# Two layers of a gated-recurrence and dilated-attention model: SwiGLU weights moved by 64 bytes in their tiles, one more pair of hidden columns computed by seven products

## The chip, the core and the metric

The kernel runs on one core of a Trainium2 chip. The metric is the device time of one launch in microseconds (us), lower is better. TensorE (PE) multiplies matrices and loads their stationary operand (PEld), VectorE (DVE) and ScalarE (ACT) do elementwise work, GpSimd (POOL) some additions and reductions, and SyncE (SP) issues most transfers from memory.

## The reference

512 tokens of width 1024 go through two layers in float32. Layer 0 mixes tokens by a gated recurrence (HGRN2), layer 1 by dilated attention; each is followed by a SwiGLU feed-forward part (FFN) with 2816 hidden columns.

```
cond = silu(c)
for layer in range(2):
    mod = cond @ ada_w[layer] + ada_b[layer]
    sh1, sc1, g1, sh2, sc2, g2 = split(mod, 6)
    u = rms_norm(h, norm_g[layer, 0]) * (1 + sc1) + sh1
    y = hgrn2_mixer(u, ...) if layer == 0 else dilated_attention_mixer(u, ...)
    h = h + (1 + g1) * rms_norm(y, norm_g[layer, 1])
    u = rms_norm(h, norm_g[layer, 2]) * (1 + sc2) + sh2
    gate, up = split(u @ ffn_w_in[layer], 2)          # 1024 -> 2 x 2816
    y = (silu(gate) * up) @ ffn_w_out[layer]          # 2816 -> 1024
    h = h + (1 + g2) * rms_norm(y, norm_g[layer, 3])
```

## The kernel before

Every float32 operand is split into two parts, hi (the value rounded by ScalarE's cast) and lo (the rest, by a VectorE subtraction). `three` (L401 to L404) replaces one product by three matmuls on the same PSUM bank: hi by hi, hi by lo, lo by hi. The first operand is the stationary one (the weights), the second the moving one (the tokens, `uh` and `ul`, tiles of 128 x 8 x 512).

**Weights.** A `Stream` loads the weights in the order in which they are needed, through SP's queue: 1 MB pieces [128, 2048] into two `raw` buffers. `process_to` casts each into a `hi` tile (L83, ACT) and subtracts into a `lo` tile (L84, DVE); there are three buffers of each. Between the weights the stream carries pieces of `ada_w` (the table that `cond` is multiplied with). Most of these are summed by VectorE (L241, L243), the total over the partitions by POOL's all-reduce (L245); `row_fin` (L290, L291) then needs two short rows, `ada_b` and `norm_g` (loads of L59). For layer 0's values 2 to 4 PE does it instead (L221), with a tile `tiled_cond` of copies of `cond` as its moving operand, which DVE fills at L1300. An equal tile, `cond_tiles`, exists earlier in the start stage, in a pool that has been closed by then.

**FFN.** The 2816 hidden columns are 22 blocks f of 128. `PLAIN = (4, 2)` says how many pairs of blocks each layer computes in the plain way: a pair is 4 products (gate and up, two blocks each) with 24 matmuls of 512 tokens, so 96 matmuls. Silu is L876, the product with up L877. The other blocks (f 8 to 21 in layer 0, f 4 to 21 in layer 1) go through `seven_products`: gate and up of one f are seen as a 2 x 2 block matrix and computed with seven block products (Strassen-like) instead of eight, each a `run` of 12 matmuls of 256 tokens, 84 matmuls for an f.

- Three of the runs use three quarters of the raw weights (tiles R: `spare` for even f, tiles of the stream's `hi` and `lo` rings for odd f), with the token parts B11, T4 and B21. R is cast by L746 on ACT, its lo part is L750 on DVE.
- Four use sums of the quarters (tiles Sm), with t2, T3, t1 and B22. The sums are made by L754 (POOL), L758 and L762 (DVE), cast by L770 (ACT, two halves) and subtracted by L774 (DVE, two halves).
- B11, B21 and B22 are slices of `uh`/`ul`; t1, T3, T4 and t2 are the token sums, in tiles `th`/`tl`, which `token_sums` makes once per layer (L711 to L718).
- L799, L803, L809, L814 on DVE and L833, L843, L810 on ACT combine the seven results.

One f is 4 transfers of 256 KB (L56, "quarters"). Those of the first f take the `raw` buffer that becomes free two pieces earlier.

**Order of the work.** Inside `tc.manual_schedule(engines=ORDERED)` PE, ACT, DVE and POOL run the instructions in the order of the code; `seven_products` is written so. Elsewhere a scheduler picks the order, so also for `token_sums`, for the plain pairs, for the casts of the stream's weights and for the FFN's second product.

**Places in SBUF.** As the program is laid out, the tiles `uh`, `ul`, `hi`, `lo` and `spare` begin 64 bytes past a multiple of 128 bytes in each partition, `th` and `tl` on a multiple of 128 bytes.

Of the kernel before, what the change touches and what calls it, by code (L numbers as in the profile page):

```python
# [15 lines left out]
P = 128  # L16
# [14 lines left out]
C3 = float(np.float32(TWO_PI - C1 - C2))  # L31
MAGIC = 12582912.0


# [116 lines left out]
def block_kernel(tc, x, c, positions, ada_w, ada_b, norm_g, hgrn_w_in, lower, hgrn_norm_g, hgrn_w_out,  # L151
# [6 lines left out]
    with ExitStack() as ctx:  # L158
# [49 lines left out]

        tiled_cond = []
        by_pe = lambda l, v: l == 0 and v in (2, 3, 4)  # L210

        def ada_groups(l, v, hf, kq):


            def run(raw):
                if kq == 0:
                    accs[l, v, hf] = bank("mm")
                ps, r = accs[l, v, hf], V4(raw)
                for k in range(4):
                    j = slice(32 * k, 32 * k + 32)  # L220
                    pe.matmul(ps[j], tiled_cond[0][:, kq * 4 + k], r[:, k], start=kq == 0, stop=kq == 1,  # L221
                              tile_position=(0, 32 * k))
# [118 lines left out]

        PLAIN = (4, 2)

# [362 lines left out]
        def token_sums(th, tl, room):  # L706

            q = lambda a, k: a[:, k // 2 * 4:k // 2 * 4 + 4, k % 2 * 256:k % 2 * 256 + 256].bitcast(F32)
            t = [room[:, 2 * k:2 * k + 2].rearrange("p a (b n) -> p (a b) n", b=2) for k in range(4)]
            for k in (0, 1, 3, 2):  # L710
                dve.tensor_add(t[k], q(uh, k), q(ul, k))  # L711
            dve.tensor_sub(t[0], t[0], t[1])
            dve.tensor_sub(t[1], t[3], t[1])
            dve.scalar_tensor_tensor(t[3], t[0], -1.0, t[3], op0=OP.mult, op1=OP.subtract)
            dve.scalar_tensor_tensor(t[2], t[3], -1.0, t[2], op0=OP.mult, op1=OP.subtract)
            for k in (3, 0, 2, 1):
                act.copy(th[:, k], t[k])
                dve.tensor_sub(tl[:, k], t[k], th[:, k].bitcast(F32))  # L718

        def seven_products(fs, mid, sgp, spare, th, tl):  # L720
# [5 lines left out]
            u_of = lambda r, c: [(uh[:, r * 4 + k, c * 256:c * 256 + 256], ul[:, r * 4 + k, c * 256:c * 256 + 256]) for k in range(4)]  # L726
            t_of = lambda i: [(th[:, i, k], tl[:, i, k]) for k in range(4)]
            B11, B21, B22 = u_of(0, 0), u_of(1, 0), u_of(1, 1)
# [14 lines left out]
            def r_hi(i):  # L743
                if i < len(fs):
                    raw[i] = st.quarters()
                    act.copy(places(i)[0][0][:, 0:1536], raw[i][:, 512:])  # L746

            def r_lo(i):
                hi, lo = places(i)[0]
                dve.tensor_sub(lo[:, 0:1536], raw[i][:, 512:], hi[:, 0:1536].bitcast(F32))  # L750

# [26 lines left out]

            def run(ps, w, k, us):
                for kt in range(4):  # L780
                    a = slice(k * 512 + kt * P, k * 512 + (kt + 1) * P)
                    three(ps, w[0][:, a], w[1][:, a], *us[kt], kt == 0, kt == 3)

            def runs(i):
# [8 lines left out]
                run(half(2, 1), Sm, 2, T3)  # L793
                run(half(2, 0), Sm, 1, t1)
                run(half(3, 0), Sm, 3, B22)

# [367 lines left out]
        with tc.manual_schedule(engines=ORDERED):  # L1164
# [6 lines left out]
            cT = fresh(sp, [P, 8], "cT", 1)  # L1171
            cond_tiles = sp.tile([P, KT, 32], F32, name="cond_tiles")
            busy(4)
# [124 lines left out]
        sc = cx.enter_context(tc.tile_pool(name="h_briefest", bufs=1))  # L1298
        tiled_cond.append(sc.tile([P, KT, 32], F32, name="tiled_cond"))
        dve.tensor_scalar(tiled_cond[0], cond.unsqueeze(2).broadcast_to((P, KT, 32)), 1.0 / 32, None, op0=OP.mult)  # L1300
        causal = sc.tile([P, P], F32, name="causal")
# [170 lines left out]

        cx.close()
        first = mixer_out(oT, otp, (8,), gates.pop((0, 2)), 0, "left", lambda: None)

# [260 lines left out]
```

## Time and profile before

| what | value |
|---|---|
| median of three runs | 1528.15 us (1527.87 to 1528.92) |
| profiled execution: its time | 1527.97 us |
| profiled execution: its span | 1526.3 us, so 1.67 us lie around it |
| granted TensorE clock | 0.998 |
| PE busy | 1507.9 us (99%) |
| DVE busy | 1010.5 us (66%) |
| ACT busy | 685.2 us (45%) |
| POOL busy | 233.3 us (15%) |
| matmuls | 8871 |

In a timeline row stand the start in us, the duration, the engine, the line, the operation, output <- inputs, how many, and in brackets the idle time before it with what ended it. Names are those of the program without buffer numbers. A matmul's duration covers its whole passage through the array; since they overlap, the pace is read from one start to the next. An SPq row of several issues shows the time from the first issue to the last.

### The profile page before, as it was taken

To read this page: it belongs to the slowest core of one execution; us is meant where nothing else is said; L and a number is where in the kernel's file an instruction comes from. 1 tells how busy PE (TensorE), PEld (TensorE's weight loads), DVE (VectorE), ACT (ScalarE), POOL (GpSimd) and SP (SyncE) were. 2 spreads that over 40 slices of the span, in tenths; PEclk is the share of its full clock that TensorE was granted. 3 is DMA by queue.
4 is the path that set the end of the run, shared out by engine and by line. 5 is a ranking of instruction groups with operands and counts; after the bars stand their busy time and mean duration, and the time that the engine had idled before them with its cause. 6 is when DMAs were issued, how large, how long until landed. Compare 5 with 4: busy or idle time off the path is not lost.

```text
span 1526.3 us, 22515 instructions
## 1 busy us (share of the span) xinstructions
PE 1507.9 (99%) x8871; PEld 1322.7 (87%) x8871; DVE 1010.5 (66%) x1737; ACT 685.2 (45%) x1091; POOL 233.3 (15%) x204
## 2 busy tenths in 40 slices
PE   8999999999999999999999999999999999999998
PEld 6777888898899988889888888988888999999886
DVE  4587866487688887462567686335656868888633
ACT  4433443362344533362456664245645534444231
POOL 1011210031122211140010111010002212221100
PEclk9999999999999999999999999999999999999999
DMA  9654443126433356414534433443202333334531
GB/s 307 184 160 135 156 138 111 56 84 207 125 109 106 108 198 221 151 55 139 165 99 133 130 111 111 138 111 84 83 30 82 106 89 110 104 107 151 186 117 55
DMA packets 203352, 192.77 MB, mean 126 GB/s; under 512 B 6584, under 2 KB 162416, under 8 KB 203248
## 3 DMA queue, kind: packets, MB, share of 16 engines
q1 hardware_dynamic: 201712, 190.87, 40.6%
q8 instruction: 69, 1.13, 0.3%
q0 software_dynamic: 1024, 0.13, 0.2%
q10 hardware_dynamic: 512, 0.35, 0.1%
q14 instruction: 35, 0.29, 0.1%
HBM read 189.17 MB, written 2.16 MB: 125 GB/s over the span
## 4 chain that ended last, share of the span: by engine, by line
PE 90%; DVE 3%; ACT 2%; issue 2%; DMA 1%; POOL 1%; DVEq 0%; POOLq 0%; ACTq 0%
PE ps_mm L402 20%; PE ps_mm L404 20%; PE ps_mm L403 20%; PE ps_b L402 3%; PE ps_b L404 3%; PE ps_b L403 3%; PE ps_a L404 3%; PE ps_a L403 3%; PE ps_a L402 3%; PE ps_mm L1140 1%; PE ps_a L1140 1%; PE ps_mm L221 1%; PE ps_a L1587 1%; PE ps_b L1140 1%; PE ps_a L1569 1%
## 5 line engine op out<-in xcount | busy, mean ns | idle before, releaser
L402 PE MATMUL ps_mm<-uh,hi 128*128 128x512 f32 (+1 forms) x816 | 309.8, 380 | 0.0
L404 PE MATMUL ps_mm<-uh,lo 128*128 128x512 f32 (+1 forms) x816 | 308.3, 378 | 0.0
L403 PE MATMUL ps_mm<-ul,hi 128*128 128x512 f32 (+1 forms) x816 | 307.4, 377 | 0.0
L84 DVE TENSOR_TENSOR lo<-raw,hi 128x2048 fp32r<-128x2048 f32 x78 | 186.0, 2384 | 168.0 <-ACT hi L83 167.8
L83 ACT CAST hi<-raw 128x2048 fp32r<-128x2048 f32 x78 | 148.8, 1908 | 172.0 <-DMA raw<-in_ffn_w_out_dram 53.4
L402 PEld LDWEIGHTS ps_mm<-uh,hi 128*128 128x128 f32 x816 | 153.8, 188 | 35.2 <-issue 8.4
L404 PEld LDWEIGHTS ps_mm<-uh,lo 128*128 128x128 f32 x816 | 153.8, 188 | 27.2
L403 PEld LDWEIGHTS ps_mm<-ul,hi 128*128 128x128 f32 x816 | 153.8, 189 | 26.2
L402 PE MATMUL ps_mm<-hi,oh 128*128 128x512 f32 x240 | 94.0, 392 | 0.0
L403 PE MATMUL ps_mm<-lo,oh 128*128 128x512 f32 x240 | 93.5, 390 | 0.0
L243 DVE SCALAR_TENSOR_TENSOR shared<-raw,cond,shared 128x512 f32<-128x512 f32 x98 | 73.4, 749 | 29.1 <-DMA raw<-in_ada_w_dram 27.4
L770 ACT CAST hiq<-raw 128x1024 fp32r<-128x1024 f32 x64 | 64.4, 1050 | 62.8 <-DVE raw L758 62.8
L245 POOL PARTITION_ALL_REDUCE shared<-shared x14 | 47.5, 3396 | 288.7 <-DVE shared L243 288.6
L404 PE MATMUL ps_mm<-hi,ul 128*128 128x512 f32 x192 | 76.0, 396 | 0.0
L403 PE MATMUL ps_mm<-lo,uh 128*128 128x512 f32 x192 | 75.9, 396 | 0.0
L774 DVE TENSOR_TENSOR loq<-raw,hiq 128x1024 fp32r<-128x1024 f32 x64 | 75.5, 1220 | 0.6 <-ACT hiq L770 0.6
L402 PE MATMUL ps_mm<-hi,uh 128*128 128x512 f32 x192 | 74.6, 396 | 0.0
L404 PE MATMUL ps_mm<-hi,ol 128*128 128x512 f32 x176 | 68.5, 389 | 0.0
L754 POOL TENSOR_TENSOR raw<-raw 128x512 f32<-128x512 f32 x32 | 52.5, 1642 | 99.4 <-DVE spare L750 42.4
L758 DVE TENSOR_TENSOR raw<-raw 128x1024 f32<-128x1024 f32 x32 | 39.2, 1226 | 36.7 <-POOL raw L754 36.5
L402 PE MATMUL ps_a<-hi,oh 128*128 128x512 f32 x152 | 59.7, 392 | 0.0
L403 PE MATMUL ps_a<-lo,oh 128*128 128x512 f32 x152 | 59.2, 390 | 0.0
(403 smaller groups left out, 3716.0 us busy)
## 6 DMA issues: line engine op xcount, KB each, us to landing
raw<-in_ada_w_dram SPq DMA_DIRECT2D x40, 1024.0 KB, 5.2
raw<-in_ffn_w_in_dram SPq DMA_DIRECT2D x128, 256.0 KB, 4.3
raw<-in_attn_w_in_dram SPq DMA_DIRECT2D x48, 512.0 KB, 4.9
raw<-in_ffn_w_out_dram SPq DMA_DIRECT2D x22, 1024.0 KB, 4.8
raw<-in_hgrn_w_in_dram SPq DMA_DIRECT2D x12, 1024.0 KB, 5.6
raw<-in_ffn_w_in_dram SPq DMA_DIRECT2D x12, 1024.0 KB, 5.1
raw<-in_attn_w_in_dram SPq DMA_DIRECT2D x12, 1024.0 KB, 5.2
first<-in_ada_w_dram SPq DMA_DIRECT2D x14, 512.0 KB, 7.6
```

Source lines behind the costliest of these rows:

```text
L83: self.nc.scalar.copy(hi, t)
L84: self.nc.vector.tensor_sub(lo, t, hi.bitcast(F32))
L243: dve.scalar_tensor_tensor(a, r[:, k], sc, a, op0=OP.mult, op1=OP.add)
L245: pool.partition_all_reduce(a, a, P, bass.bass_isa.ReduceOp.add)
L402: pe.matmul(ps, ah, bh, start=start, stop=False)
L403: pe.matmul(ps, ah, bl, start=False, stop=False)
L404: pe.matmul(ps, al, bh, start=False, stop=stop)
L754: pool.tensor_add(r[:, 2], r[:, 2], r[:, 0])
L758: dve.tensor_tensor(r[:, 0:2], r[:, 0:3:2], r[:, 1:2].broadcast_to((P, 2, 512)), op=OP.add)
L770: act.copy(hi, src)
L774: dve.tensor_sub(lo, src, hi.bitcast(F32))
L1140: pe.matmul(vbanks[hf, t], a, w, start=e == 0 and which == 0, stop=e == KT - 1 and which == 2)
```

## The change

1. The three raw quarters R begin R0 = 16 floats (64 bytes) later in their tiles (L746, L750, the three `run` calls), so on a multiple of 128 bytes. The token sums move from `th`/`tl` into `sums` (t1, T3, t2, on a multiple of 128 bytes) and `fourth` (T4, 64 bytes past one). `uh`, `ul` and Sm stay, 64 bytes past one. So in six of the seven runs of an f the stationary operand and the moving one now differ by 64 modulo 128, and only B22's are equal; before, they differed in four (T4, t2, T3, t1) and were equal in the three with `uh` (B11, B21, B22).
2. `PLAIN` becomes (3, 2): layer 0 has three plain pairs and 16 blocks by seven products (14 before).
3. `token_sums` stands inside `manual_schedule`, so the engines run it in the order of the code.
4. `tiled_cond` and its instruction go; `cond_tiles` lives on in a pool of its own until the first mixer is done, and L221 reads that.

```
+R0 = 16
+        tcx = ctx.enter_context(ExitStack())
+        cond_tiles = tcx.enter_context(tc.tile_pool(name="tiled", bufs=1, side="right")).tile([P, KT, 32], F32, name="cond_tiles")
...
-                    pe.matmul(ps[j], tiled_cond[0][:, kq * 4 + k], r[:, k], start=kq == 0, stop=kq == 1,
+                    pe.matmul(ps[j], cond_tiles[:, kq * 4 + k], r[:, k], start=kq == 0, stop=kq == 1,
...
-        PLAIN = (4, 2)
+        PLAIN = (3, 2)
...
-                act.copy(th[:, k], t[k])
-                dve.tensor_sub(tl[:, k], t[k], th[:, k].bitcast(F32))
+                act.copy(th[k], t[k])
+                dve.tensor_sub(tl[k], t[k], th[k].bitcast(F32))
...
-                    act.copy(places(i)[0][0][:, 0:1536], raw[i][:, 512:])
+                    act.copy(places(i)[0][0][:, R0:R0 + 1536], raw[i][:, 512:])
...
-                dve.tensor_sub(lo[:, 0:1536], raw[i][:, 512:], hi[:, 0:1536].bitcast(F32))
+                dve.tensor_sub(lo[:, R0:R0 + 1536], raw[i][:, 512:], hi[:, R0:R0 + 1536].bitcast(F32))
...
-            def run(ps, w, k, us):
+            def run(ps, w, o, us):
...
-                    a = slice(k * 512 + kt * P, k * 512 + (kt + 1) * P)
+                    a = slice(o + kt * P, o + (kt + 1) * P)
...
-                run(half(0, 0), R, 0, B11)
-                run(half(3, 1), R, 1, T4)
-                run(half(1, 0), R, 2, B21)
+                run(half(0, 0), R, R0, B11)
+                run(half(3, 1), R, R0 + 512, T4)
+                run(half(1, 0), R, R0 + 1024, B21)
                 run(half(1, 1), Sm, 0, t2)
...
-                    spare = [qp.tile([P, 3 * 512], F32R, name=f"spare{l}{k}") for k in range(2)]
-                    qp.tile([P, 112], F32, name=f"pad_q{l}")
-                    th = qp.tile([P, 4, 4, 256], F32R, name=f"th{l}")
-                    tl = qp.tile([P, 4, 4, 256], F32R, name=f"tl{l}")
+
+                    spare = [qp.tile([P, R0 + 1536 + n], F32R, name=f"spare{l}{n}") for n in (112, 96)]
+                    three_t = qp.tile([P, 2 * 3072 + 16], F32R, name=f"sums{l}")
+                    fourth_t = qp.tile([P, 2 * 1024], F32R, name=f"fourth{l}")
+                    K4 = lambda t: t.rearrange("p (k n) -> p k n", k=4)
+                    sums = [[K4(three_t[:, o + k:o + k + 1024]) for k in (0, 1024, 2048)] for o in (0, 3072)]
+                    for k in range(2):
+                        sums[k].insert(2, K4(fourth_t[:, k * 1024:(k + 1) * 1024]))
+                    th, tl = sums
...
-                            token_sums(th, tl, midt[:, NF - 8:])
+                            with tc.manual_schedule(engines=ORDERED):
+                                token_sums(th, tl, midt[:, NF - 8:])
...
-        tiled_cond.append(sc.tile([P, KT, 32], F32, name="tiled_cond"))
-        dve.tensor_scalar(tiled_cond[0], cond.unsqueeze(2).broadcast_to((P, KT, 32)), 1.0 / 32, None, op0=OP.mult)
```

Lines of the code after the change have numbers one to eight higher (L84 becomes L85, L746 L748, L774 L776, L877 L884).

On SP's queue, at the end of layer 0's plain pairs, the order before, from the last piece of `ada_w` for this stage:

```order
L65 DMA raw_3149<-in_ada_w_dram 128x4x512
L65 DMA raw_3210<-in_ffn_w_in_dram 128x8x256
L65 DMA raw_3217<-in_ffn_w_in_dram 128x8x256
L59 DMA raw_3223<-in_ada_b_dram 128x512
L59 DMA raw_3223<-in_norm_g_dram 128x512
L56 DMA raw_3280<-in_ffn_w_in_dram 128x4x128 x4
L56 DMA raw_3343<-in_ffn_w_in_dram 128x4x128 x4
```

And after:

```order
L66 DMA raw_3153<-in_ada_w_dram 128x4x512
L60 DMA raw_3214<-in_ada_b_dram 128x512
L60 DMA raw_3214<-in_norm_g_dram 128x512
L57 DMA raw_3222<-in_ffn_w_in_dram 128x4x128 x4
L57 DMA raw_3229<-in_ffn_w_in_dram 128x4x128 x4
```

The two 1 MB loads of the fourth pair are gone, and the quarters of the first f follow the rows at once; their `raw` buffer is the one of the `ada_w` piece in the first row.

On VectorE, around layer 0's token sums (L711 to L718, now L713 to L720), before:

```order
L713 TENSOR_TENSOR mid_3029<-mid_3029 128x1024
L243 SCALAR_TENSOR_TENSOR shared<-raw_2752,cond,shared 128x512
L718 TENSOR_TENSOR tl_3040<-mid_3029,th_3039 128x1024
L877 TENSOR_TENSOR mid_3029<-ps_mm_2757,sg_3044 128x512
L714 SCALAR_TENSOR_TENSOR mid_3029<-mid_3029 128x1024
L243 SCALAR_TENSOR_TENSOR shared<-raw_2752,cond,shared 128x512
L718 TENSOR_TENSOR tl_3040<-mid_3029,th_3039 128x1024
L84 TENSOR_TENSOR lo_3070<-raw_2922,hi_3069 128x2048
L715 SCALAR_TENSOR_TENSOR mid_3029<-mid_3029 128x1024
L718 TENSOR_TENSOR tl_3040<-mid_3029,th_3039 128x1024
L243 SCALAR_TENSOR_TENSOR shared<-raw_3067,cond,shared 128x512
L718 TENSOR_TENSOR tl_3040<-mid_3029,th_3039 128x1024
```

And after:

```order
L715 TENSOR_TENSOR mid_3031<-mid_3031 128x1024
L884 TENSOR_TENSOR mid_3031<-ps_mm_2759,sg_3045 128x512
L716 SCALAR_TENSOR_TENSOR mid_3031<-mid_3031 128x1024
L245 SCALAR_TENSOR_TENSOR shared<-raw_2754,cond,shared 128x512
L717 SCALAR_TENSOR_TENSOR mid_3031<-mid_3031 128x1024
L85 TENSOR_TENSOR lo_3074<-raw_2924,hi_3073 128x2048
L720 TENSOR_TENSOR sums_3040<-mid_3031,sums_3040 128x1024 x2
L720 TENSOR_TENSOR fourth_3041<-mid_3031,fourth_3041 128x1024
L720 TENSOR_TENSOR sums_3040<-mid_3031,sums_3040 128x1024
L245 SCALAR_TENSOR_TENSOR shared<-raw_3071,cond,shared 128x512 x2
```

The four subtractions that fill the sums' lo parts now stand together behind the weight's subtraction (L84, now L85), ahead of the next `ada_w` piece's sums; before they were spread.

On ScalarE, at the end of layer 0's seven products, before, from the cast of the last f's R to the first weight of the FFN's second product (L83):

```order
L746 CAST hiq_3472<-raw_4676 128x1536
L810 ACTIVATE shared<-shared 128x512
L833 COPY shared<-ps_mm_4791 128x256
L770 CAST hiq_3474<-raw_4676 128x1024 x2
L843 COPY shared<-ps_mm_4793 128x256
L83 CAST hi_5018<-raw_4786 128x2048
```

And after:

```order
L748 CAST hiq_3358<-raw_4782 128x1536
L812 ACTIVATE shared<-shared 128x512
L835 COPY shared<-ps_mm_4897 128x256
L84 CAST hi_5124<-raw_4892 128x2048
L772 CAST hiq_3360<-raw_4782 128x1024 x2
L845 COPY shared<-ps_mm_4899 128x256
```

The weight's cast now stands ahead of the two casts of the last f's Sm; on VectorE its subtraction (L84, now L85) in the same way stands ahead of the two L774 (now L776) of that f. The `hi` buffer that it writes is the one that held the Sm of the f before.

More of the change, by code (lines that the diff above doesn't have):

```diff
@@ L726, in seven_products @@
             u_of = lambda r, c: [(uh[:, r * 4 + k, c * 256:c * 256 + 256], ul[:, r * 4 + k, c * 256:c * 256 + 256]) for k in range(4)]
-            t_of = lambda i: [(th[:, i, k], tl[:, i, k]) for k in range(4)]
+            t_of = lambda i: [(th[i][:, k], tl[i][:, k]) for k in range(4)]
             B11, B21, B22 = u_of(0, 0), u_of(1, 0), u_of(1, 1)
@@ L788, in runs @@
                 half = lambda n, k: b[n][:, k * 256:k * 256 + 256]
[L789 to L791 removed]
+                run(half(0, 0), R, R0, B11)
+                run(half(3, 1), R, R0 + 512, T4)
+                run(half(1, 0), R, R0 + 1024, B21)
                 run(half(1, 1), Sm, 0, t2)
[L793 to L795 removed]
+                run(half(2, 1), Sm, 1024, T3)
+                run(half(2, 0), Sm, 512, t1)
+                run(half(3, 0), Sm, 1536, B22)
             def sums_1(i):
@@ L1171, in block_kernel @@
             cT = fresh(sp, [P, 8], "cT", 1)
-            cond_tiles = sp.tile([P, KT, 32], F32, name="cond_tiles")
             busy(4)
@@ L1473, in block_kernel @@
         cx.close()
+        tcx.close()
         first = mixer_out(oT, otp, (8,), gates.pop((0, 2)), 0, "left", lambda: None)
```

1 line of the change is left out of this document (removed).

## The prediction

> **What bounds the kernel now.** I read the page's busy times first, then TensorE's timeline, its idle gaps, and the other engines' timelines beside those places that the change touches.
>
> ```profile
> PE 1507.9 (99%) x8871; PEld 1322.7 (87%) x8871; DVE 1010.5 (66%) x1737; ACT 685.2 (45%) x1091; POOL 233.3 (15%) x204
> ```
>
> TensorE is busy for 99% of the span, so time comes or goes in three ways only: fewer or shorter matmul slots, a gap of TensorE closed, or a new gap. The unit for the first is the pace from start to start in layer 0's feed-forward part.
>
> ```profile
> 339.24 0.40 PE L402 MATMUL ps_mm<-uh,hi 128*128 128x512 f32 x1
> ...
> 404.55 0.28 PE L402 MATMUL ps_mm<-uh,spare 128*128 128x256 f32 x1
> ...
> 405.98 0.29 PE L402 MATMUL ps_mm<-th,spare 128*128 128x256 f32 x1
> ...
> 407.36 0.28 PE L402 MATMUL ps_mm<-uh,spare 128*128 128x256 f32 x1
> ...
> 408.78 0.29 PE L402 MATMUL ps_mm<-th,hiq 128*128 128x256 f32 x1
> ...
> 412.88 0.28 PE L402 MATMUL ps_mm<-uh,hiq 128*128 128x256 f32 x1
> ...
> 424.06 0.28 PE L402 MATMUL ps_mm<-uh,spare 128*128 128x256 f32 x1
> ```
>
> From 339.24 to 404.55 stand three plain pairs, 3 x 96 matmuls of 512 tokens: 65.31 us, 21.77 a pair, 0.2268 a matmul, and half of it, 0.1134, is the pace that 256 tokens would have at the same rate. From 404.55 to 424.06 stand two blocks f by seven products: 19.51 us, 9.755 a block. Inside one, the runs of 12 matmuls are not alike: B11 with `uh` takes 1.43, T4 with `th` 1.38, B21 with `uh` 1.42, and the three runs t2, T3, t1 with `th` 4.10 together, 1.367 each. So `uh` costs 0.05 to 0.06 a run more than `th`, at the same shapes.
>
> **The change part by part**, against the profiled execution's 1527.97 us, which is 0.18 under the median of the runs (1528.15); I make no correction for that.
>
> *The 64 bytes.* Before, `uh` and the weights both begin 64 bytes past a multiple of 128, while `th` and the weights differ by 64. All slow runs are of the first kind and all fast ones of the second. After the change B11, T4, B21, t2, T3 and t1 are all of the second kind, B22 stays of the first. Six runs at 12 x 0.1134 = 1.361 and one at 1.43 make 9.60 for a block: 0.155 less, for the 32 blocks that the kernel has already 5.0 us less. The ends: 0, if it is `uh` itself that is slow and not its place against the weights; and what VectorE allows at the other end. VectorE's wait on TensorE in a block is the 0.20 us of L809 that is quoted with the end of the stage below, so its own round is 9.755 - 0.20 = 9.555, and 32 x 0.20 = 6.4 is the most that the pace can give. I take 5.0, since slow and fast rows part exactly along the placement. It is also close to VectorE's limit: 0.05 us of slack a block is left.
>
> The Trainium skill, "SBUF — State Buffer", section "SBUF: two separate sides", says of TensorE that it never waits on anyone for its ports, and the page's table of bandwidths gives the weight load a second, independent read port. By that, the place of the operands could not change the pace, and the sum would lack these 5.0 us. The rows above show a difference between equal shapes that the rule has no word for; that it comes from the placement no row shows, since `uh` is never seen at another place.
>
> *One more pair by seven products.* 21.77 go, 2 x 9.60 = 19.20 come: 2.57 less (2.26 less without the shift, 21.77 - 19.51).
>
> *The copies of the condition.*
>
> ```profile
> 74.79 0.39 PE L1140 MATMUL ps_b<-late,uh 128*128 128x512 f32 x1
> 76.51 1.06 PE L221 MATMUL ps_mm<-raw,tiled_cond 128*32 128x512 f32 x8 [1.33 <-DVE tiled_cond L1300]
> ```
> ```profile
> 75.83 0.39 DVE L1300 TENSOR_SCALAR tiled_cond<-cond 128x256 f32<-128x256 f32 x1
> ```
> ```profile
> 69.67 0.37 SPq L65 DMA_DIRECT2D raw<-in_ada_w_dram  x1
> ```
> ```profile
> raw<-in_ada_w_dram SPq DMA_DIRECT2D x40, 1024.0 KB, 5.2
> ```
>
> L221 waited 1.33 us for the tile that the change removes. What is late next is its own piece of `ada_w`: issued at 69.67, with 5.2 us to landing, there at 74.9, before TensorE ends the matmul of 74.79 at 75.2. So 1.3 less; the ends are 1.33 and 0.3, should that piece land 1 us late.
>
> *The start of layer 0's seven products.* Here the fourth pair was the cover.
>
> ```profile
> 368.56 0.38 SPq L65 DMA_DIRECT2D raw<-in_ada_w_dram  x1
> 369.88 7.46 SPq L65 DMA_DIRECT2D raw<-in_ffn_w_in_dram  x2
> ...
> 387.98 5.94 SPq L56 DMA_DIRECT2D raw<-in_ffn_w_in_dram  x8
> ```
> ```profile
> 393.44 1.48 ACT L746 CAST spare<-raw 128x1536 fp32r<-128x1536 f32 x1 [9.39 <-DMA raw<-in_ffn_w_in_dram]
> ```
> ```profile
> 373.84 3.11 DVE L243 SCALAR_TENSOR_TENSOR shared<-raw,cond,shared 128x512 f32<-128x512 f32 x4 [3.98 <-DMA raw<-in_ada_w_dram]
> ...
> 394.95 1.76 DVE L750 TENSOR_TENSOR spare<-raw,spare 128x1536 fp32r<-128x1536 f32 x1 [5.80 <-ACT spare L746]
> 398.13 1.23 DVE L758 TENSOR_TENSOR raw<-raw 128x1024 f32<-128x1024 f32 x1 [1.42 <-POOL raw L754]
> ...
> 400.47 1.23 DVE L774 TENSOR_TENSOR loq<-raw,hiq 128x1024 fp32r<-128x1024 f32 x1 [0.39 <-ACT hiq L770]
> 401.90 1.23 DVE L774 TENSOR_TENSOR loq<-raw,hiq 128x1024 fp32r<-128x1024 f32 x1 [0.21 <-ACT hiq L770]
> ```
> ```profile
> 396.80 1.29 POOL L754 TENSOR_TENSOR raw<-raw 128x512 f32<-128x512 f32 x1 [16.52 <-DMA raw<-in_ffn_w_in_dram]
> ```
>
> Before, R's parts were ready at 396.71 (L750) and Sm's first half at 401.70 (L774), and TensorE came to R at 404.55 and to Sm, three runs later, at 408.78: 7 us to spare. After, TensorE is through with the third pair at 339.24 + 2 x 21.77 = 382.78. The quarters now follow the `ada_w` piece of 368.56, whose `raw` buffer they take. That piece is issued when a buffer falls free; the token sums' new order puts the subtractions in a row ahead of the sums that free it, and I put that at 0.4 later (an estimate; 0 if the order costs nothing, and no more than one subtraction, 1.2), so 368.96. It lands 5.28 later (368.56 to 373.84), its four L243 take 3.11: the quarters are issued at 377.35. R is cast 5.46 after that (387.98 to 393.44): 382.81. L750 ends 3.27 after the cast's start (393.44 to 396.71): 386.08; so TensorE waits 3.3 there. Sm's first half is complete 8.26 after the cast's start (393.44 to 401.70): 391.07. TensorE, with its three runs with R, would be at Sm at 382.78 + 4.2 = 386.98 without any wait. So 4.1 more in all, R's wait included; Sm's second half, 1.43 later, then falls into the run with t2. The ends: 2.5 if the reordering costs nothing and the quarters land 1.2 sooner with no 1 MB load among them; 5.5 if the one subtraction is fully in the way and more. In this stage nobody else can start earlier: the cast, the subtraction and POOL's sum stand in a fixed order, one waiting for the other.
>
> *The end of layer 0's seven products.*
>
> ```profile
> 527.26 2.00 ACT L770 CAST hiq<-raw 128x1024 fp32r<-128x1024 f32 x2 [1.98 <-DVE raw L758]
> ...
> 531.54 1.92 ACT L83 CAST hi<-raw 128x2048 fp32r<-128x2048 f32 x1 [0.97 <-PE ps_mm L403]
> ```
> ```profile
> 528.47 2.35 DVE L774 TENSOR_TENSOR loq<-raw,hiq 128x1024 fp32r<-128x1024 f32 x2
> ...
> 531.62 0.69 DVE L809 TENSOR_TENSOR shared<-shared,ps_mm 128x512 f32<-128x512 f32 x1 [0.20 <-PE ps_mm L404]
> 533.49 2.29 DVE L84 TENSOR_TENSOR lo<-raw,hi 128x2048 fp32r<-128x2048 f32 x1 [1.18 <-ACT hi L83]
> ```
>
> L83 writes the `hi` buffer of the block before and so waits for the end of that block's runs (0.97, on PE); it used to come behind the last L770 and L774, now it stands ahead of them, and all three wait with it. With T the end of those runs: L83 T + 0.1 to 2.0, then the two casts to 3.0 and 4.0; on DVE L84 to 4.3, the first L774 to 5.45. TensorE needs that half at T + 4.3, after the last block's runs with R. So 1.1 more, between 0 (the scheduler's estimate of what comes first doesn't meet the chip's queue) and 2.4 (both halves late).
>
> *What I cost at nothing.* Layer 1's token sums also take the order of the code, but there is room:
>
> ```profile
> 1230.22 0.69 DVE L799 TENSOR_TENSOR shared<-shared,ps_mm 128x512 f32<-128x512 f32 x1 [4.99 <-PE ps_mm L404]
> ```
>
> VectorE waits 4.99 us for TensorE in the first block there, after all sums and subtractions; without that cover each subtraction out of place would cost 1.2. The longer life of one tile moves no instruction.
>
> The sum: -5.0 - 2.57 - 1.3 + 4.1 + 1.1 = -3.7, so 1527.97 - 3.7 = **1524.3 us**.
>
> **The rivals.**
>
> *The shift does nothing* (slower than before). `uh` is slow wherever it stands, for example because it lies in another part of SBUF than `th`. The Trainium skill's page "SBUF — State Buffer" (the section above) would have it so as well. Then the blocks stay at 9.755: -2.26 - 1.3 + 4.1 + 1.1 = +1.6, 1529.6 us. It decides from the point where less than 1.3 of the 5.0 us comes, 0.04 a block, since then the stalls outweigh the rest. For it: the two kinds differ by name as well as by place, and the matmuls of 512 tokens with `uh` show no loss (0.2268 is twice 0.1134). Against it: nothing else in shape or source tells the two kinds apart. Chance 0.18.
>
> *No stall at the start* of the seven products: the quarters are issued or land some 4 us earlier than I have it, which takes a `raw` buffer falling free sooner than its reader's row says. 1524.3 - 4.1 = 1520.2. For it: SP's queue is empty there after the change. Against: the buffer's last reader, L243, is bound to a landing seen 5.28 us after its issue. Chance 0.13.
>
> *VectorE sets the pace of the blocks.* Its round has 0.05 us to spare. If L750, which now writes 64 bytes further on, or POOL's L754 beside it takes longer, every one of 34 blocks is longer by that. From a round of 9.71 us (9.60 + 3.7 / 34; L750's 1.76 longer by 9%) the kernel is slower than before, at 9.80 it stands at 1524.3 + 6.8 = 1531.1. For it: the small slack. Against: L774 and L750 run at the same rate per element (1.23 for 1024, 1.76 for 1536), and both tiles' places stay on multiples of 64. Chance 0.08.
>
> **How the numbers follow.** The forecast has 0.61. About 0.2%, 3.06 us, is what a measurement of this kernel can tell from no change: faster is below 1524.9, slower above 1531.0. My forecast lies just past the first bound; of its 0.61 I give 0.41 to faster, 0.19 to no change (stalls at their upper ends, or a shift that gives only part) and 0.01 to slower. The shift that does nothing gives 0.16 to no change and 0.02 to slower, no stall 0.13 to faster, VectorE's pace 0.02 to no change and 0.06 to slower. So faster 0.54, within 0.2% 0.37, slower 0.09. The range: the lower end is the case without a stall, 1520.0, with half of that case below; the upper end 1530.2 takes in the useless shift at 1529.6 with little above it. That leaves out VectorE's pace, half of the case without a stall and some tails, some 0.2 in all.
>
> **What would show it.** Right: runs with `uh` and R at 1.36 to 1.37, a block's pace at 9.58 to 9.62, no wait at L221 over 0.1, a wait of TensorE for L752 of some 3.3 us near 383 and one for L776 of under 1, and some 1.1 us before the last block's t2. Wrong: runs B11 and B21 still at 1.42; TensorE waiting for L776 in every block (VectorE's pace); no gap between the third pair and the first block; or a stall of over 6 us there, which would mean that the quarters were held up by more than the one piece.

## The result, and the profile after

The changed kernel takes 1530.11 us (median of 20 runs, 1529.31 to 1532.18), the kernel before beside it 1528.38 (20 runs): a ratio of 1.0011 with a 95% interval of 1.0004 to 1.0018. It is slower by 1.7 us, a tenth of a per cent; the interval excludes no change, but the difference is under 0.2%. The forecast was 1524.3; the time lies in its range, next to the rival "the shift does nothing" (1529.6). The profiled execution took 1530.53, with a span of 1528.8 (before 1527.97 and 1526.3).

The busy times on the page of after:

```profile
PE 1508.3 (99%) x8943; PEld 1326.6 (87%) x8943; DVE 1020.5 (67%) x1750; ACT 687.5 (45%) x1099; POOL 237.8 (16%) x208
```

TensorE's timeline of after, two blocks of layer 0:

```profile
407.37 0.28 PE L404 MATMUL ps_mm<-uh,spare 128*128 128x256 f32 x1
...
408.79 0.28 PE L404 MATMUL ps_mm<-fourth,spare 128*128 128x256 f32 x1
...
410.20 0.28 PE L404 MATMUL ps_mm<-uh,spare 128*128 128x256 f32 x1
...
411.62 0.29 PE L404 MATMUL ps_mm<-sums,hiq 128*128 128x256 f32 x1
...
415.71 0.28 PE L404 MATMUL ps_mm<-uh,hiq 128*128 128x256 f32 x1
...
426.89 0.28 PE L404 MATMUL ps_mm<-uh,spare 128*128 128x256 f32 x1
```

Two blocks take 19.52, 9.76 each; before it was 9.755. The runs with `uh` and R still take 1.42, although the weights now lie 64 bytes away from `uh` modulo 128. T4 even went from 1.38 to 1.41, and the three runs with the sums stayed at 4.09 together. The 5.0 us of the forecast are not there.

The copies of the condition, on TensorE:

```profile
74.95 1.06 PE L223 MATMUL ps_mm<-raw,cond_tiles 128*32 128x512 f32 x8
```

No wait is left, and the row stands 1.56 earlier than before (76.51). The wait is 1.33 of that; in `p1_pair_only` (below), which leaves this part alone, the row stands at 76.09, so some tenths differ from one execution to the next.

Now the start of layer 0's seven products. Timelines of SP, ScalarE, VectorE and POOL of after:

```profile
368.16 0.38 SPq L66 DMA_DIRECT2D raw<-in_ada_w_dram  x1
...
376.43 36.04 SPq L57 DMA_DIRECT2D raw<-in_ffn_w_in_dram  x19
```
```profile
382.04 1.47 ACT L748 CAST spare<-raw 128x1536 fp32r<-128x1536 f32 x1 [10.85 <-DMA raw<-in_ffn_w_in_dram]
```
```profile
383.54 1.76 DVE L752 TENSOR_TENSOR spare<-raw,spare 128x1536 fp32r<-128x1536 f32 x1 [2.36 <-ACT spare L748]
...
388.59 1.22 DVE L760 TENSOR_TENSOR raw<-raw 128x1024 f32<-128x1024 f32 x1 [2.69 <-POOL raw L756]
...
390.93 2.36 DVE L776 TENSOR_TENSOR loq<-raw,hiq 128x1024 fp32r<-128x1024 f32 x2 [0.39 <-ACT hiq L772]
```
```profile
376.50 3.23 POOL L247 PARTITION_ALL_REDUCE shared<-shared  x1 [16.87 <-DVE shared L245]
387.29 1.27 POOL L756 TENSOR_TENSOR raw<-raw 128x512 f32<-128x512 f32 x1 [7.56 <-DMA raw<-in_ffn_w_in_dram]
```

And TensorE there:

```profile
383.56 0.58 PE L404 MATMUL ps_mm<-uh,spare 128*128 128x256 f32 x1 [2.19 <-ACT spare L748]
...
385.35 0.58 PE L406 MATMUL ps_mm<-uh,spare 128*128 128x256 f32 x1 [1.00 <-DVE spare L752]
...
392.22 0.39 PE L406 MATMUL ps_mm<-sums,loq 128*128 128x256 f32 x1 [0.21 <-DVE loq L776]
```

TensorE was free at 383.56 - 2.19 = 381.37. The three runs with R (4.2) and the two matmuls before the one that needs `loq` (0.24) would bring it there at 385.8; it came at 392.22, so the stall is 6.4 us. Two things filled it. POOL began its first addition 2.0 after VectorE had finished with R (385.30), and 7.56 after its own all-reduce. And the matmuls themselves ran at half pace, as the windows of after show:

```profile
core 0: us, PE busy (x) PEld busy (x) DVE busy (x) ACT busy (x) POOL busy (x), PEclk, DMA share, GB/s
381.00:385.00 4.00, 1.17 (x4) 0.50 (x2) 1.64 (x2) 1.47 (x1) 0.00 (x0) 0.80 0.74 210
385.00:390.00 5.00, 4.65 (x21) 4.65 (x22) 2.27 (x4) 0.15 (x1) 1.27 (x1) 0.50 0.30 90
```

A mean granted clock (PEclk) of 0.80 over the 4 us from 381 is 1.6 us at 0.50, so the clock had fallen by 383.4, within the gap of 2.19 us. The 21 matmuls from 385 to 390, behind the gap of 1.00, go at 0.213 us each instead of the 0.113 to 0.118 of a block without gaps.

The end of layer 0's seven products, on ScalarE, VectorE and TensorE:

```profile
534.38 1.91 ACT L84 CAST hi<-raw 128x2048 fp32r<-128x2048 f32 x1 [3.39 <-PE ps_mm L405]
536.19 1.99 ACT L772 CAST hiq<-raw 128x1024 fp32r<-128x1024 f32 x2
```
```profile
536.32 2.29 DVE L85 TENSOR_TENSOR lo<-raw,hi 128x2048 fp32r<-128x2048 f32 x1 [2.06 <-ACT hi L84]
538.53 2.35 DVE L776 TENSOR_TENSOR loq<-raw,hiq 128x1024 fp32r<-128x1024 f32 x2
```
```profile
539.81 0.38 PE L406 MATMUL ps_b<-sums,loq 128*128 128x256 f32 x1 [0.91 <-DVE loq L776]
```

The weight's cast waits and the last f's casts wait behind it, as forecast: 0.91 us.

Where the span went, by the start of the same matmuls in both traces: 1.6 gained up to the first pair (339.24 to 337.67); 5.6 lost inside layer 0's feed-forward part (its end 675.37 to 679.39, so from 1.6 ahead to 4.0 behind); 0.9 regained in the attention that follows, for which I found no cause, and 0.6 before layer 1's feed-forward part. That leaves 2.5, the difference of the two spans. Of the 5.6, the stall (6.4), the end (0.9) and the pair (21.77 - 19.52 = 2.25 saved) explain 5.05; the other half microsecond I couldn't place.

### The profile page after: what moved, and what is told of

It is laid out like the page before. It is cut to its first block, busy times and chain, and to the rows that moved or that the text cites. A ratio compares the mean times of both kernels' runs of the same rounds, so it can differ in the third digit from the quotient of the medians.

```text
span 1528.8 us, 22711 instructions
## 1 busy us (share of the span) xinstructions
PE 1508.3 (99%) x8943; PEld 1326.6 (87%) x8943; DVE 1020.5 (67%) x1750; ACT 687.5 (45%) x1099; POOL 237.8 (16%) x208
## 4 chain that ended last, share of the span: by engine, by line
PE 88%; DVE 4%; issue 3%; DMA 2%; ACT 2%; POOL 1%; SPq 0%; POOLq 0%; DVEq 0%; ACTq 0%
PE ps_mm L404 19%; PE ps_mm L406 19%; PE ps_mm L405 19%; PE ps_b L406 3%; PE ps_b L404 3%; PE ps_b L405 3%; PE ps_a L406 3%; PE ps_a L405 3%; PE ps_a L404 3%; PE ps_mm L1148 1%; DMA raw<-in_ffn_w_in_dram 1%; PE ps_a L1593 1%; PE ps_a L1148 1%; PE ps_a L1575 1%; PE ps_mm L223 1%
## 5 line engine op out<-in xcount | busy, mean ns | idle before, releaser
L404 PE MATMUL ps_mm<-uh,hi 128*128 128x512 f32 (+1 forms) x784 | 297.1, 379 | 0.0
L406 PE MATMUL ps_mm<-uh,lo 128*128 128x512 f32 (+1 forms) x784 | 295.8, 377 | 0.0
L405 PE MATMUL ps_mm<-ul,hi 128*128 128x512 f32 (+1 forms) x784 | 294.7, 376 | 0.0
L85 DVE TENSOR_TENSOR lo<-raw,hi 128x2048 fp32r<-128x2048 f32 x76 | 179.2, 2358 | 165.4 <-ACT hi L84 165.2
L84 ACT CAST hi<-raw 128x2048 fp32r<-128x2048 f32 x76 | 145.1, 1909 | 175.8 <-DMA raw<-in_ffn_w_out_dram 57.0
L404 PEld LDWEIGHTS ps_mm<-uh,hi 128*128 128x128 f32 x784 | 147.7, 188 | 34.0 <-issue 8.4
L406 PEld LDWEIGHTS ps_mm<-uh,lo 128*128 128x128 f32 x784 | 147.7, 188 | 25.9
L405 PEld LDWEIGHTS ps_mm<-ul,hi 128*128 128x128 f32 x784 | 147.8, 188 | 25.0
L772 ACT CAST hiq<-raw 128x1024 fp32r<-128x1024 f32 x68 | 68.2, 1049 | 70.8 <-DVE raw L760 69.6
L776 DVE TENSOR_TENSOR loq<-raw,hiq 128x1024 fp32r<-128x1024 f32 x68 | 80.1, 1218 | 0.4 <-ACT hiq L772 0.4
L756 POOL TENSOR_TENSOR raw<-raw 128x512 f32<-128x512 f32 x34 | 54.6, 1607 | 94.6 <-DVE loq L752 44.5
L806 POOL TENSOR_TENSOR shared<-shared 128x256 f32<-128x256 f32 x34 | 28.0, 822 | 205.1 <-DVE shared L805 205.1
```

The costliest lines, as they stand in the source:

```text
L84: self.nc.scalar.copy(hi, t)
L85: self.nc.vector.tensor_sub(lo, t, hi.bitcast(F32))
L404: pe.matmul(ps, ah, bh, start=start, stop=False)
L405: pe.matmul(ps, ah, bl, start=False, stop=False)
L406: pe.matmul(ps, al, bh, start=False, stop=stop)
L756: pool.tensor_add(r[:, 2], r[:, 2], r[:, 0])
```

## The experiments

Times are medians, ratios are against the kernel before on the same chip, with 95% intervals.

**The parts one by one.** Each part alone, put into the kernel before: the shift of the weight quarters (`m3_shift_only`), the fourth pair of layer 0 (`p1_pair_only`), the condition (`p2_cond_only`) and the order of the token sums (`p3_order_only`).

```diff
 m3:  places(i)[0][0][:, 0:1536]  ->  places(i)[0][0][:, R0:R0 + 1536], R0 = 16, and the new tiles for the sums
 p1: -        PLAIN = (4, 2)
     +        PLAIN = (3, 2)
 p2:  tiled_cond (filled at L1300)  ->  cond_tiles, kept until the first mixer is done
 p3: +                            with tc.manual_schedule(engines=ORDERED):
                                      token_sums(th, tl, midt[:, NF - 8:])
```

> The kernel before with the first part of the change alone (quarters 64 bytes higher, the sums' new tiles with T4 64 past a multiple of 128). Theory (the moving operand's own place): T4 slows from 1.38 to 1.41, B11 and B21 stay at 1.42, the block stays within 0.02 of 9.755; no change within 0.5 us. The prediction's reading (the places must differ): 9.60 a block, -5 us.

1528.35 us (11 runs), ratio 1.0001 [0.9992, 1.0010]. TensorE's timeline, from one block to the second after it:

```profile
407.19 0.28 PE L403 MATMUL ps_mm<-uh,spare 128*128 128x256 f32 x1
...
426.70 0.28 PE L403 MATMUL ps_mm<-uh,spare 128*128 128x256 f32 x1
```

Two blocks take 19.51: the same 9.755 as before. The shift alone is worth nothing. It does change single runs: over six pairs of blocks in layer 0 the median of B11 goes from 1.440 to 1.413, B21 and B22 lose 0.005 and 0.003, and T4 goes from 1.379 to 1.414, which takes all of that back.

> The kernel before with PLAIN (3, 2) alone. Theory (the extra pair's 2.3 us are more than eaten by the start of the seven products): POOL's first addition can't start until about 7.6 us after its all-reduce, so Sm's first half comes at some 392.5, TensorE would be there at 387.2; 5.4 us of stall with R's wait, 0.9 at the end, less 2.26: +4 us. Rival (the prediction's price for the stalls, 4.1 and 1.1, without the shift): +2.9 us, with POOL's addition right behind L750.

1532.52 us, 1.0027 [1.0016, 1.0039]: 4.1 slower. The pair by itself costs more than it saves. The traced execution is the shortest of the seven (1531.19); its POOL timeline:

```profile
376.00 3.23 POOL L245 PARTITION_ALL_REDUCE shared<-shared  x1 [19.11 <-DVE shared L243]
386.17 1.28 POOL L754 TENSOR_TENSOR raw<-raw 128x512 f32<-128x512 f32 x1 [6.93 <-DMA raw<-in_ffn_w_in_dram]
```

Here too POOL's first addition begins 6.9 us after the all-reduce. Two more rows of after bear on that. The first is POOL's next change, from additions to an all-reduce, where it waited for nothing that the profile shows; the second is from the view of line L756, two instructions right behind the all-reduce of 376.50:

```profile
562.43 4.00 POOL L247 PARTITION_ALL_REDUCE shared<-shared  x1 [7.65 <-issue]
```
```profile
L756 POOLq MODIFY_POOL_CONFIG  x2: 88/88/88, 379.7 to 379.7; - x2
```

The row of 562.43 has 7.59 and 7.58 in `q1_first_sum_dve` and `q2_kept_busy` below. In all sixteen traces POOL's next own instruction came 6.86 us or more after such a MODIFY_POOL_CONFIG, except at the program's start. So the price of about 7 us goes with POOL's change of work, in both directions.

The gaps of TensorE at this place are 0.55, 1.29, 0.71 and 0.76 us, and the granted clock stays at 1.00 in this execution. In after the first gap is longer, because TensorE arrives earlier by the condition's gain; that this alone brings the half pace is not shown.

> The kernel before with the one tile of copies of the condition alone. Both theories: TensorE's wait of 1.33 at the first L221 goes, -1.3 to -1.6 us, and it stays so to the end. Rival (another wait takes its place before the layer's end): no change.

1526.67 us, 0.9986 [0.9977, 0.9994]: 1.8 faster.

> The kernel before with the token sums in the order of the code alone. Theory: no wait of TensorE depends on it with four plain pairs, 0 within 0.5 us. Rival (the order delays the stream's casts): slower by up to 1.2.

1527.46 us, 0.9990 [0.9982, 0.9999]: 1.0 faster, where nothing was expected. Part of it is in the view of the waits, on TensorE's wait for `xn` (the columns are total, times, longest):

```profile
PE ps_b L481 <- DVE xn L475: 2.3, 2, 1.4
```

Before the longest was 2.1, so 0.6 went ahead of layer 1's feed-forward part. The same row of after is also at 1.4; in the kernels here with the old order it is 2.0 to 2.2, with the new one 1.2 to 1.6. Together: +4.1 - 1.8 - 1.0 + 0 = +1.3, against a measured +1.7.

**The start of the seven products.** Two theories of what holds the stall up: POOL's late addition, or TensorE's half pace. The first kernel (`q1_first_sum_dve`) gives the first block's addition to VectorE, the second (`q2_kept_busy`) also lets TensorE multiply constants in the gap.

```diff
 q1 (on the changed kernel)
-                pool.tensor_add(r[:, 2], r[:, 2], r[:, 0])
+                (dve if i == 0 else pool).tensor_add(r[:, 2], r[:, 2], r[:, 0])
 q2 (q1, and ahead of layer 0's first block)
+                    for _ in range(14):
+                        pe.matmul(idle_b[:, 0:P], ones, ones, start=True, stop=True)
```

> The changed kernel with the first block's addition on VectorE instead of POOL (each layer's block 0). Theory one (POOL's 7.6 us after its all-reduce are what Sm waits for, and TensorE's half pace after the gap isn't binding): Sm's first half at 390.1 instead of 392.1, -2 us. Theory two (TensorE's half pace from 385.4 to 390.2 sets when it reaches Sm, 391.6): only -0.6 us. Rival (the fourth quarter really landed that late): no change, VectorE waits until 387.3 for it.

1529.66 us, 1.0009 [1.0000, 1.0018]; only 0.45 under the changed kernel. The addition on VectorE, then the windows and TensorE:

```profile
385.35 0.69 DVE L756 TENSOR_TENSOR raw<-raw 128x512 f32<-128x512 f32 x1
```
```profile
385.00:391.00 6.00, 5.63 (x26) 5.63 (x27) 5.55 (x7) 3.19 (x3) 0.00 (x0) 0.50 0.24 69
```
```profile
392.23 0.29 PE L404 MATMUL ps_mm<-sums,hiq 128*128 128x256 f32 x1
```

VectorE adds at 385.35 without a wait, so the quarter that it reads was there: the DMA that the row of POOL names as its releaser wasn't what held POOL. Sm's first half was then ready at about 390.1, but TensorE at clock 0.50 came to it only at 392.23. Each of the two causes alone holds TensorE until about 392.2, so in this execution taking away one gains nothing. Its mean clock is 0.995: six of q1's eleven executions have 0.995 to 0.997 and a median of 1530.9, five have 0.998 and 1528.78. The half pace may thus be missing in some of them; only the traced one shows where the clock fell.

> The changed kernel with the first addition on VectorE and 14 unused matmuls of 128 columns (ones by ones, into a free bank) in TensorE's gap before layer 0's first block, so that TensorE isn't idle there. Theory (the half pace after the gap is what is left of the stall): the runs with R at 1.4 instead of 2.5, Sm reached at some 390.2 instead of 392.2, -2 us against the run without the 14. Rival (the half pace comes from the operands or from something else than the gap): no change.

1528.77 us, 0.9999 [0.9991, 1.0008]; 1.3 under the changed kernel. The windows and TensorE again:

```profile
385.00:390.00 5.00, 5.00 (x44) 4.85 (x43) 4.97 (x6) 3.20 (x3) 0.00 (x0) 1.00 0.20 59
```
```profile
389.02 0.39 PE L406 MATMUL ps_mm<-sums,loq 128*128 128x256 f32 x1
```

The clock stays at 1.00, 44 matmuls run where 21 did, and Sm is reached 3.2 earlier than in after. The end of the feed-forward part moves from 679.39 to 676.17, the same 3.2; on the median 1.3 arrive. The scheduler put about half of the fourteen matmuls at 326 us, where they cost TensorE time for nothing. Against q1, where POOL's wait is gone as well, the same matmul stands 3.5 earlier (392.48 there), and the median is 0.9 lower, which is not clear of the intervals. So in the traced executions the half pace costs about 3 us once POOL's wait is gone, and it goes when the gap is filled.

**Why the shift does nothing.** The theory left was that the place of both operands sets the pace, by another rule than the forecast's. `m1_uh_low` moves `uh` and `ul` to a multiple of 128 bytes; `m2_all_low` then all moving operands and R; `m4_all_high` moves the sums 64 bytes past one, like `uh` and the weights.

```diff
 m1 (on the kernel before): lb and omlb are allocated behind uh and ul
 m2 (m1 and): R0 = 16, the new tiles, and 16 floats more ahead of `fourth`
 m4 (on the kernel before)
-                    qp.tile([P, 112], F32, name=f"pad_q{l}")
+                    qp.tile([P, 96], F32, name=f"pad_q{l}")
```

> The kernel before with uh and ul 64 bytes lower in SBUF, on a multiple of 128; nothing else moves, weights stay 64 past one. Theory (a run of 256 tokens is fast when its moving operand begins on a multiple of 128 bytes, wherever the weights stand): all seven runs of a block at 1.36 to 1.38 us, the block at 9.53 to 9.56 instead of 9.755, so about 6.4 us less over 32 blocks, and some 2 us less from the other 384 matmuls of 256 tokens with uh: about -8 us. Rival (uh is slow wherever it stands): no change, 9.755 a block.

1538.74 us, 1.0063 [1.0051, 1.0076]: 10.7 slower where 8 less were expected. TensorE's timeline in layer 0, then in layer 1, from one block to the second after it:

```profile
408.60 0.28 PE L402 MATMUL ps_mm<-uh,spare 128*128 128x256 f32 x1
...
428.38 0.28 PE L402 MATMUL ps_mm<-uh,spare 128*128 128x256 f32 x1
```
```profile
1277.44 0.28 PE L402 MATMUL ps_mm<-uh,spare 128*128 128x256 f32 x1
...
1296.48 0.28 PE L402 MATMUL ps_mm<-uh,spare 128*128 128x256 f32 x1
```

The same instructions, on places that are alike modulo 128: 9.89 a block in layer 0 (every run 1.41), 9.52 in layer 1 (every run 1.36). Places modulo 128 alone don't decide it. Besides, the matmuls of 512 tokens with `uh` went from 227 to 233 ns from start to start, and that is what makes the kernel slower. (In the traced execution 1.7 us of the 10.7 are lost at half clock, at a mean of 0.57 over the 4 us from 1198.)

> As the run with uh and ul on a multiple of 128, with all four token sums there too, and with the raw quarters moved by 64 bytes as in the change, so that moving and stationary operand of the three runs with R both begin on a multiple of 128. Theory (the moving operand's own place): the same as without moving the quarters, 9.53 to 9.56 a block, about -8 us. Rival (the two operands' places must differ, as the prediction had it): the three runs with R at 1.42 each, a block at 9.70, about -4 us.

1548.35 us (4 runs), 1.0126 [1.0111, 1.0141], blocks of 9.94 in both layers: neither the 9.53 to 9.56 of the theory nor the 9.70 of the rival.

> The kernel before with the token sums th and tl 64 bytes lower, so also 64 past a multiple of 128, like uh and the weights. Theory (the moving operand's own place): all seven runs at 1.42 to 1.44, a block at 9.95 to 10.05, +6 to +9 us over 32 blocks. Rival (uh is slow because of what it is or where in SBUF it lies, not modulo 128): no change.

1535.20 us, 1.0044 [1.0031, 1.0056]. TensorE's timeline, two blocks:

```profile
404.36 0.28 PE L402 MATMUL ps_mm<-uh,spare 128*128 128x256 f32 x1
...
424.32 0.28 PE L402 MATMUL ps_mm<-uh,spare 128*128 128x256 f32 x1
```

Blocks of 9.98: with all operands 64 bytes past a multiple of 128 every run is slow (1.42 to 1.44), 32 x 0.225 = 7.2, which is all of the 7 us measured.

`m5_uh_low_other_entry` is m1 with four matmuls of constants more; the scheduler put them into the first pair, 79 us ahead of the blocks.

```diff
 m5 (m1, and ahead of layer 0's blocks)
+                    for _ in range(4):
+                        pe.matmul(idle_b[:, 0:P], ones, ones, start=True, stop=True)
```

> The kernel with uh and ul on a multiple of 128 throughout, and four unused matmuls (ones by ones, about 1 us) between layer 0's last plain pair and its first block by seven products. No operand moves. Theory (the same operands have two paces, 113 and 118 ns, and the entry to a stretch decides): layer 0's 14 blocks may go from 9.90 to 9.52, -5.3 us + 1. Rival (layer 0's pace is set by its places or by what runs beside it): 9.90 as before, +1 us.

1535.70 us (5 runs, 1532.64 to 1536.53), 1.0038 [1.0025, 1.0050]. TensorE's timeline:

```profile
330.31 1.05 PE L829 MATMUL ps_b<-ones 128*128 128x128 f32 x8
...
409.28 0.28 PE L402 MATMUL ps_mm<-uh,spare 128*128 128x256 f32 x1
...
428.33 0.28 PE L402 MATMUL ps_mm<-uh,spare 128*128 128x256 f32 x1
```

Layer 0's blocks now take 9.52 instead of 9.89, with no operand moved. One trace of each kernel shows this; all five times of m5 lie under all five of m1 (1537.54 to 1539.22). The four matmuls also shift which of the two `ps_b` banks comes next, but the blocks of even f, which use neither, change alike (118 to 113 ns a matmul). q2 shows both paces in one execution, for the run B21 on the same tiles, in the first block behind the stall and in the third:

```profile
387.31 0.28 PE L404 MATMUL ps_mm<-uh,spare 128*128 128x256 f32 x1
...
388.67 0.28 PE L404 MATMUL ps_mm<-sums,hiq 128*128 128x256 f32 x1
...
407.00 0.28 PE L404 MATMUL ps_mm<-uh,spare 128*128 128x256 f32 x1
...
408.42 0.29 PE L404 MATMUL ps_mm<-sums,hiq 128*128 128x256 f32 x1
```

The run takes 1.36 and then 1.42. So one and the same layout has two paces, and what ran before bears on which of them comes; what it is that decides, no run here shows.

**A version that is faster.** `b0_cond_order` keeps the two parts that gained, the condition and the order of the sums. `b1_low_in_ffn1` and `f1_low_in_ffn1_256` add to it that layer 1's feed-forward part alone has `uh` and `ul` on a multiple of 128 bytes, the one place where m1 had gained; f1 keeps all other tiles on their places modulo 256. `f5_entry_only` is b0 with four matmuls of constants more in each layer, with nothing moved; the scheduler put them into each layer's first pair, at 326 and 1189 us.

```diff
 f1 (b0, and; in b1 the rooms are 16 floats longer, uh lies at 0 and ul at 16, in layer 1's feed-forward part uh at 16 and ul at 0)
-        uh = base.tile([P, KT, S], F32R, name="uh")
-        ul = base.tile([P, KT, S], F32R, name="ul")
+        uh_room = base.tile([P, KT * S + 64], F32R, name="uh")
+        ul_room = base.tile([P, KT * S + 64], F32R, name="ul")
+        at_floats = lambda t, o: t[:, o:o + KT * S].rearrange("p (k n) -> p k n", k=KT)
+        uh, ul = at_floats(uh_room, 0), at_floats(ul_room, 0)
 ... ahead of layer 1's feed-forward part
+        uh, ul = at_floats(uh_room, 48), at_floats(ul_room, 48)
```

> The kernel before with the one tile of copies and the token sums in the order of the code, four plain pairs and the old places. Theory (the parts add up): -1.8 - 1.0 = -2.8 us. Rival (both take the same slack): -1.8.

1525.52 us, 0.9982 [0.9973, 0.9991], 3.1 less. The two gains add up in the traced spans too (2.6 less, against 1.8 and 0.8 for p2 and p3), though the interval doesn't exclude the rival's -1.8.

> As the run with the copies and the order, and layer 1's FFN alone reads and writes uh and ul on a multiple of 128 bytes (both tiles 64 bytes longer). Theory (the stretch falls into the 113 ns pace as it did in layer 1 with uh low throughout): the 18 blocks at 9.52 instead of 9.755, -4.2, the two plain pairs at 233 ns instead of 227, +1.2: -3 us against the run with the copies and the order. Rival (the pace is chosen at the entry and this one falls to 118): 18 blocks at 9.90, +2.6 +1.2 = +3.8 us.

1527.83 us, 0.9999 [0.9988, 1.0009]. The blocks of layer 1 do run at 9.52, but the 512-token matmuls of the mixers went from 227 to 232 ns. In this kernel `ul` and the tiles behind it lie 128 bytes further on, against `uh`, which stays; only the next run tests whether that is the reason.

> As the run with the copies and the order, and layer 1's FFN alone has uh and ul 192 bytes further on (on 128 modulo 256, like th); the rooms of both tiles are longer by 256 bytes, so that every other tile keeps its place modulo 256. Theory (the distance modulo 256 counts, and 128 was what slowed the run with rooms longer by 64 bytes): the mixers' matmuls of 512 tokens back at 227 ns, layer 1's 18 blocks at 9.52: -3 us against the run with the copies and the order, about 1522.5. Rival (places modulo 128 are what counts, the slow mixers there had another cause): the mixers again at 232 ns, no gain against the kernel before.

1521.43 us, 0.9961 [0.9949, 0.9972]: faster than both kernels, and 4.1 under b0. The pace gives 18 x 0.235 = 4.2, and the two plain pairs at 233 ns take back 0.6. TensorE's timeline in layer 1:

```profile
1221.84 0.28 PE L405 MATMUL ps_mm<-uh,spare 128*128 128x256 f32 x1
...
1240.89 0.28 PE L405 MATMUL ps_mm<-uh,spare 128*128 128x256 f32 x1
```

Two blocks in 19.05, and the mixers are back at 227 ns. Eleven of its twelve executions lie between 1520.95 and 1524.29; one took 1530.84, and has no trace. The slow pace of m1's layer 0 in these 18 blocks would be 18 x 0.37 = 6.7 of the 9.4 us; whether it was that stays open.

> As the run with the copies and the order, with four unused matmuls (ones by ones, 1 us) ahead of each layer's first block; all places as before. Theory (the entry decides only until the next change of operands, and uh and th alternate here): blocks at 9.755 again after the first, +2 us for the eight matmuls. Rival (the entry decides for the whole stretch): 9.52 a block, -7.5 + 2 us.

1527.98 us, 0.9994 [0.9986, 1.0003], 2.5 over b0, and blocks of 9.76 in both layers as in b0: where runs with `uh` and with the sums lie on different places, the four matmuls change no pace and only cost.

## Why the prediction was wrong

- **The 64 bytes: forecast -5.0, measured 0.** This is the step that failed: "slow and fast rows part exactly along the placement". They did, in two kinds of rows of one trace; it was a correlation of two things that differed in name, tile and place alike. m3 gives the term as 1.0001 [0.9992, 1.0010]: B11 got faster, T4 slower by as much. The rival's own reason ("`uh` is slow wherever it stands") fell as well: in m1's layer 1 and in f1 `uh` runs at 1.36. What the runs put in its place: the pace of a run depends on where both operands lie and, on some places, on how the stage was entered. Starts of 256-token matmuls lie 113, 118 or 120 ns apart, those of 512 tokens 227 or 233; moving and stationary both 64 bytes past a multiple of 128 gave 118 to 120 (m4); T4 at the one place in SBUF ran 118 in m3 and after, 113 in q2's first block. Which mechanism does it, no run here shows. The Trainium skill's "SBUF — State Buffer", section "SBUF: two separate sides", has TensorE waiting on nobody for its ports. That gave the right time for this shift, but by luck, since two changes cancel; m1, m4 and b1, where the same shapes change by 2 to 5% with the place alone, are against it as a rule.
- **VectorE's own round: forecast 9.555, which left 0.05 of slack.** Wrong too: f1 runs its blocks at 9.52 without TensorE waiting. The 0.20 us of wait that this was worked out from is no measure of an engine's round where it waits at one of many rows only.
- **The start of the seven products: forecast 4.1, measured 6.4**, mis-sized in two pieces. TensorE came at 381.37, 1.4 earlier than the 382.78 used: the condition's gain was counted in full and then spent waiting here. And Sm's first half came 1.1 later than forecast (392.2 against 391.07), although R came 0.8 earlier: POOL's addition had been taken at its duration, with 16.52 us of idle time before it hiding that POOL needs about 7 us between an all-reduce and its next addition (7.56 in after, 6.93 in p1). The Trainium skill's "GPSIMD Engine Reference", section 2.1 "Instruction dispatch", has such a price: the first call into freshly loaded code pays about 6 us. The rows here agree in kind and lie 1 to 1.6 above. The half pace was not foreseen either, and q1 shows that it alone would have held TensorE until the same 392.2. The sign that the prediction gave, a stall of over 6 us, did come, but not for its reason: the quarters were issued at 376.43, 0.9 earlier than forecast.
- **The pair, the condition and the end were right**: -2.57 forecast, or -2.26 without the shift, and -2.25 by the paces (21.77 - 19.52); -1.3 forecast, -1.56 by the trace and -1.8 by p2; +1.1 forecast, 0.91 measured.
- **The order of the sums, forecast at nothing** (0.4 late at the start): p3 gained 1.0, of which 0.6 shows as a shorter wait for `xn`; and the `ada_w` piece behind the sums was issued at 368.16, 0.4 earlier than before. Whether the order delays it stays open: in p1, with the old order, it was issued at 367.48.
- With 0 in place of -5.0, 6.4 in place of 4.1, and the 1.0 of the order, and the pair, condition and end as measured, the prediction's own sum is -2.25 - 1.6 + 6.4 + 0.9 - 1.0 = +2.45, and the two spans differ by 2.5. The 1.0 is p3's time; with the 0.6 that the traces show, the sum is +2.85, and the half microsecond without a place and the 0.9 regained without a cause bring it to +2.45. So the agreement of the first sum is chance. Luck, too, is how close the rival's 1529.6 came: its start was 2.3 too low, its condition and order 1.3 too high.

## What to carry to other kernels

Two kinds of rows in one trace that differ in pace and in several attributes at once are no evidence for any one of them: move that attribute alone in a small kernel before building on it. When work that hid a start-up is removed, price everything that started under its cover, each engine's change from one kind of work to another and TensorE's clock after the gap among it, and do not book a gain that lies ahead of a stall in the same stage as well as the stall. Parts that gain alone can be kept without those that lose: the two small edits here (b0) were worth 3 us, and the pair that went with them cost 4.

## What the hardware showed that I had not expected

- Equal matmuls on equal places ran at two paces: 9.52 and 9.89 us a block in two kernels that differ in four matmuls 79 us earlier (m5 and m1), and 1.36 and 1.42 us a run in one execution (q2). m1's two layers, with places alike modulo 128, have the same two paces, and each layer of m1 and m5 kept its pace to its end.
- Moving a tile by 64 bytes changed the pace of 512-token matmuls by 2.6% (227 to 233 ns in m1); a shift of 128 bytes between operands did as well (227 to 232 in b1), and 256 did not (f1).
- POOL's change between an all-reduce and additions took 6.9 to 7.7 us, in both directions (p1, after, q1, q2).
- A gap of 2.19 us brought TensorE's granted clock to 0.50 before the gap had ended (after, from 383.4 to 390.2). In q1 two gaps of 1.57 and 1.29 with two matmuls between them did so within the second, from 384.7; gaps of 0.55 and 1.29 at the same place (p1) didn't. A gap of 2.18 ahead of layer 1's feed-forward part was followed by a fall in m1 (mean clock 0.57 from 1198 to 1202) and by none in m5 (1.00 from 1192 to 1200), so the length of the gap alone doesn't decide. The Trainium skill, "TensorE: Matmul & The Clock Gate", Part 1 "What's actually happening", puts the fall behind a whole idle window of about 3.4 us. Here no single gap was that long.
